# A hybrid attention trunk on one core: PSUM banks, squares, splits and token loads between the first feed-forward and the second attention

## The chip, the cores and the metric

The kernel runs on one core of a Trainium2 chip. The time is the device time of one execution in microseconds (us); lower is better. The core's engines work in parallel, each on its own list of instructions, strictly in the order in which they were issued: PE (matrix products, writes to the eight banks of PSUM), DVE, ACT and POOL (elementwise work), and SP, which only issues transfers (DMA). An instruction that depends on another engine waits at the head of its engine's list, and everything behind it waits too.

## The reference, cut to what matters

Two layers, each an attention and a gated feed-forward with a convolution, on 1024 latent tokens and 256 context tokens of width 1024. Only the passage from the end of layer 0 to the attention of layer 1 matters here:

```python
x = x + gt2 * conv_ffn(h, ...)                     # end of layer 0
h  = modulate(rmsnorm(x, g_attn[i]), sh1, sc1)     # layer 1: norm over 1024 features, scale and shift
hc = modulate(rmsnorm(ctx, g_attn[i]), sh1c, sc1c)
q, k, v    = attn_inputs(h, w_in, gq, gk, n_kv)             # products with the QKV weights, norm of q and k
_, k_c, v_c = attn_inputs(hc, w_in, gq, gk, n_kv, with_q=False)
o = sliding_window_attention(apply_rope(q), apply_rope(k), v, k_c, v_c, sink)
```

All of it is float32. The kernel keeps that accuracy by splitting every factor into a high part (rounded to the multiplier's format) and a low part (the difference), and by adding three products: high by high, high by low, low by high. So each operand costs a copy to the high part, mostly on ACT (`hi`), and a subtraction for the low part, on DVE or POOL (`lo`).

## The kernel before, in words

**Who sets the order.** Each phase is planned as a list of operations by the class `Sched`: an operation names its engine, a guessed duration, what it reads and writes, a `key` (the lower goes first among those that are ready) and the buffers that it takes and releases (`acq`, `rel`). `run()` plays this through with guessed durations and latencies and then issues all instructions in the order found; `InOrder` ties each engine to it. An operation with `port=True` on DVE is not planned to overlap one on POOL. Nothing is decided on the chip: a bad guess shows as a wait. The first feed-forward (`ffn(0, ...)`, whose last part is planned in `plan_next`) and the second attention are planned separately, one after the other. The second begins its plan at time 0 with what the first left; `NREADY` is the guess of when the sums of squares of the second token half are there.

**Tiling.** Features lie on the 128 partitions in eight tiles `k`, tokens along the free axis in two halves of 512 (halves 0 and 1) and the 256 context tokens. The second half is finished last.

**End of the feed-forward.** The last products of the down-projection accumulate in four PSUM banks (`dn`), finished one after another by the last 24 matmuls. DVE adds each bank, scaled, into two tiles of the residual (`xn<-dn`, eight instructions of 128x512, `plan_ev`); each result is written to memory (`x_dram<-xn`, `plan_xd`) and squared on ACT (`sq`), and DVE adds the eight squares into `sums`. Meanwhile four pieces of the context's key and value weights arrive (`ckv`, 512 KB each, into the ring `raw` of three buffers) and are split (`whi` on ACT, `wlo` on DVE).

**Start of the second attention.** A new set of PSUM tiles is laid over the same eight banks (`s` three, `pt` two, `mm` two, `pv` one), in the order in which they are first asked for. PE first computes the context's keys and values (`plan_ctx_kv`: 48 matmuls `mm<-whi,h1chi` of 128x512), then the mean square of the second half (`mp`, `pt<-invd,sums`), then the QKV products of four 128-token blocks of the first half (96 matmuls of 128x384, `mm<-whi,h1hi`, `plan_sw_qkv`), whose weights come in four pieces `slab` (384 KB, also in the ring `raw`, split like the others), then those of four blocks of the second half. For the second half `plan_norm` computes the factor 1/sqrt of the mean square (`n1v` DVE, `n1y` POOL, Newton steps on DVE), spreads it over a diagonal tile (`S<-idr,n1y`), has PE broadcast it (`bc`, `pt<-S,ones`), copies it out of PSUM (ACT), multiplies the tokens by it (`t<-x,modc,S`, eight on DVE), adds the shift and rounds (`h1hi<-t`, ACT), and takes the low part (`n1lo`, eight on DVE). The tokens of that half come back from memory (`x<-x_dram`, four transfers of 512 KB).

Each block's product is copied from its bank by ACT into one of two buffers `qraw`; q and k are normed from it (`qsq` ACT, `qv` DVE, `qy` POOL, `qt`, `qy`, `qn` DVE), which frees the buffer. The `mm` banks are two, so the product of block n+2 waits for the copy of block n. Score products (`s`), softmax and the products with V (`pv`) of one head group then run between the QKV products of the next.

Of the kernel before, what the change touches and what calls it, by code (L numbers as in the profile page):

```python
# [11 lines left out]
F32 = mybir.dt.float32  # L12
# [5 lines left out]
P = 128  # L18
D = 1024
KT = 8  # L20
# [206 lines left out]
def trunk_kernel(ctx, tc, xperm, xseq, cc, wmod, bmod, gnorm, na_wqkv, na_gq, na_gk, na_bias, na_wo,  # L227
# [87 lines left out]
    def lo_part(nm, dt=F32R):  # L315
        return hpool.tile([P, 2, 512], dt, tag="hlo", name=nm, bufs=8)
# [319 lines left out]
    def plan_norm(sc, l, psa, wk, sums, x, hl, key):  # L636
# [5 lines left out]
        if l == 0:  # L642
            for k in range(KT):
                def sq(e, k=k):
                    if k:
                        B["sq"] = wk.tile([P, 512], F32, tag="ptlo", name="sq", bufs=PTB)
                    act.activation(B["sq"] if k else sums[:, :n], x[:, k, :], AF.Square)

                def add(e, k=k, B2=B):
                    ENG[e].tensor_tensor(out=sums[:, :n], in0=sums[:, :n], in1=B2["sqs", k], op=ALU.add)  # L650

                def sq2(e, k=k, f=sq):
                    f(e)
                    B["sqs", k] = B.get("sq")
                sc.op("act", t_act(n), sq2, reads=[("x1", k)], writes=[K("sq", k)] if k else [K("sums")], key=key,
                      acq=[("ptlo", K("sq", k), 1)] if k else ())
                if k:
                    sc.op(("pool", "dve"), (t_pool(n), t_dve(n)), add, reads=[K("sq", k), K("sums")], writes=[K("sums")],
                          key=key, rel=[K("sq", k)])
        else:  # L660
            sc.op("x", NREADY, lambda e: None, writes=[K("sums")], key=key - 1)

        def mp(e):
            B["mp"] = psa("pt", F32)
            for i in range(nt):
                pe.matmul(B["mp"][:, i:i + 1], sums[:, i * P:(i + 1) * P], invd, start=True, stop=True)
        sc.op("pe", 0.4, mp, reads=[K("sums")], writes=[K("mp")], key=key, acq=[("pt", K("mp"), 1)], rel=["sums1"])

# [25 lines left out]
        sc.op("pe", 0.86, bc, reads=[K("dg")], writes=[K("bcp")], key=key, acq=[("pt", K("bcp"), 1)], rel=[K("dg")])  # L694
# [4 lines left out]
        sc.op("act", t_actp(n), bs, reads=[K("bcp")], writes=[K("bc")], key=key, acq=[("S", K("bc"), KT)], rel=[K("bcp")])  # L699
        los = []  # L700
        for k in range(KT):
            hi = hl[0][:, k, :]

            def mul(e, k=k):
                B["t", k] = wk.tile([P, 512], F32, tag=("pthi", "ptlo")[k % 2], name="t", bufs=PTB)
                dve.scalar_tensor_tensor(out=B["t", k][:, :n], in0=x[:, k, :], scalar=modc[:, l, 0, 1, k:k + 1], in1=B["bc"][:, :n],
                                         op0=ALU.mult, op1=ALU.mult)
            sc.op("dve", t_dve(n), mul, reads=[K("bc"), ("x1", k)], writes=[K("t", k)], key=key, rel=[K("bc")],
                  acq=[(("pthi", "ptlo")[k % 2], K("t", k), 1)])

            def hif(e, k=k, hi=hi):
                act.activation(hi, B["t", k][:, :n], AF.Identity, bias=modc[:, l, 0, 0, k:k + 1])
            sc.op("act", t_act(n), hif, reads=[K("t", k)], writes=[K("hi", k)], key=key)

            def lof(e, k=k, hi=hi):
                if k % 2 == 0:
                    hl[1].tiles[k // 2] = lo_part("n1lo")
                dve.scalar_tensor_tensor(out=hl[1][:, k, :], in0=B["t", k][:, :n], scalar=modc[:, l, 0, 0, k:k + 1],
                                         in1=hi.bitcast(F32), op0=ALU.add, op1=ALU.subtract)
            los.append((k, lof))  # L720
            if k % 2 == 0:
                continue
            for k, lof in los[-2:]:
                sc.op("dve", t_dve(n), lof, reads=[K("hi", k), K("t", k // 2 * 2 + 1)], writes=[(f"h{l}", 1, k)], key=key, rel=[K("t", k)])

# [245 lines left out]
    NWAIT = (2, 3, 4)  # L971
    NREADY = 7.0
    NPRE = 3
# [276 lines left out]
    def ffn(l, opj, xt1, todo):  # L1250
# [756 lines left out]
        if not last:  # L2007
            plan_next(sc, KS, xn, bank, x_tile, plan_sums, plan_bc, plan_t, plan_hilo, u_done)
        sc.run()
# [13 lines left out]

    def plan_next(sc, KS, xn, bank, x_tile, plan_sums, plan_bc, plan_t, plan_hilo, u_done):

# [65 lines left out]
        plan_sums("n1", 512, lambda k: xn(1, k), lambda k: ("xn", 1, k), lambda k: KS[5],  # L2091
                  lambda k: [("xnt", 1, k // 2)], sums, "sq")
        for i in range(4):
# [10 lines left out]
            def lo(e, i=i):  # L2104
                dve.tensor_tensor(out=CW[i][1], in0=CW[i, "r"], in1=CW[i][0].bitcast(F32), op=ALU.subtract)
            sc.op("dma", 1.8, load, reads=[("dw", 4, FT // 2 - 4, "r")], writes=[("slr", i)], key=KS[5] - 4,
                  acq=[("raw", ("slr", i), 2)])
            sc.op("act", t_act(1024), hi, reads=[("slr", i), ("dw", 4, FT // 2 - 1, "wl", 0)],
                  writes=[("slh", i)], key=key, acq=[("w", ("slw", i), 1)], rel=[("slr", i)])
            sc.op("dve", t_dve(1024) + 0.03, lo, reads=[("slr", i), ("slh", i)], writes=[("sll", i)], key=key, rel=[("slr", i)])  # L2110

# [22 lines left out]
    def plan_ctx_kv():  # L2134
# [3 lines left out]
        for i in range(4):  # L2138
            def mm(e, i=i):
                for tt in range(2):  # L2140
                    if i == 0:
                        acc[tt] = psa("mm", F32)
                    sl = slice(tt * P, tt * P + P)
                    for k in (2 * i, 2 * i + 1):
                        wh, wl = [a[:, k % 2 * 512:k % 2 * 512 + 512] for a in CW[i]]
                        for m, (a, w) in enumerate(((hh, wh), (hl, wh), (hh, wl))):
                            pe.matmul(acc[tt], a[:, k, sl], w, start=(k == 0 and m == 0), stop=(k == KT - 1 and m == 2))
            sc.op("pe", 12 * t_pe(512), mm, writes=[("ckv", "acc")], key=-300,
                  acq=[("mm", ("ckv", "acc", tt), 1) for tt in range(2)] if i == 0 else (), rel=[("cw", i)])
        for tt in range(2):  # L2150
            def cp(e, tt=tt):
                R[tt] = wk.tile([P, 672], F32, tag="S", name="S", bufs=SBUFS)
                act.activation(R[tt][:, :512], acc[tt], AF.Copy)
            r = ("ckv", "raw", tt)
            sc.op("act", t_actp(512), cp, reads=[("ckv", "acc")], writes=[r], key=-250, acq=[("S", ("ckv", "S", tt), 4)],
                  rel=[("ckv", "acc", tt)])
# [88 lines left out]
    def plan_sw_qkv(n):  # L2245
# [14 lines left out]
        plan_rstd(sc, key, J, c0, nh, wk, 320)  # L2260
        vk, qk = ("v", g, tt), ("q", g, tt)
# [17 lines left out]
        sc.op("dve", t_dve(nh * DH), qn, reads=[K("raw"), K("y")], writes=[K("qn")], key=key,  # L2279
              acq=[("qn", K("qn"), 2)], rel=[K("raw")])  # L2280
# [179 lines left out]

    for j in range(0, KT, 2):
        dma.dma_start(xs[1].tiles[j // 2], x_dram[:, (KT + j) * 512:(KT + j + 2) * 512].rearrange("p (k t) -> p k t", k=2))
    h[1] = [hpool.tile([P, KT, 512], F32R, tag="hhi", name="h1hi", bufs=2), Parts([None] * 4, 2)]
    sc.hold("raw", "sums1", 1)
    for i in range(4):
        sc.hold("w", ("cw", i), 1)
    plan_ctx_kv()
    plan_norm(sc, 1, psa, wk, sums1, xs[1], h[1], -100)
    for g in range(NKV):
# [167 lines left out]
```

## Time and profile before

| | |
|---|---|
| three executions | 2819.53, 2819.89, 2821.8 us; median 2819.89 |
| profiled execution | 2819.35 us, of which the traced span is 2817.6 us |
| granted clock of PE over the span | 0.995 of full speed |
| DVE, ACT, POOL busy | 2288.3 (81%), 1687.3 (60%), 394.4 us (14%) |

The passage lies between 1655 and 1720 us of the span. In the timeline a row gives the start, the length, the engine, the operation as out<-in with its tile names, the shape, the number of instructions merged into the row, and in brackets how long the engine sat idle before it and what ended that. "SPq" is the issuing of a transfer. A wait is put down to one releaser, the one that came last by the profile. In the table of windows each row is a stretch of time with each engine's busy time, PE's granted clock, the share of time that the DMA engines were busy, and GB/s.

### The profile page before, as it was taken

What the parts mean: (1) busy time and instruction counts of PE and PEld (TensorE: products, weight loads), DVE (VectorE), ACT (ScalarE), POOL (GpSimd) and SP (SyncE); (2) the same over time, 40 slices, a digit from 0 to 9 for tenths busy, and PEclk for the clock granted to TensorE, in tenths of its full rate; (3) what the DMA queues carried; (4) which work ended last, traced back from release to release, by engine and by line L of the source; (5) the groups of instructions that cost most, each with busy time, mean ns of one, the idle gap of its engine ahead of it and who ended that gap; (6) DMA issues with size and microseconds to landing.
All of it is one profiled execution on the core that took longest, in us unless ns stands there. A gap on an engine that the chain in (4) does not pass through costs nothing. (4 is left out here: it accounts for less than half of the span.)

```text
span 2817.6 us, 45649 instructions
## 1 busy us (share of the span) xinstructions
PE 2758.1 (98%) x16205; PEld 2427.5 (86%) x16205; DVE 2288.3 (81%) x5013; ACT 1687.3 (60%) x3312; POOL 394.4 (14%) x652
## 2 busy tenths in 40 slices
PE   6999999999999999999999999999999999999999
PEld 5999999999889987777788878999987788888887
DVE  7888878889688687778797788888988888888757
ACT  5877777778456554444454457888864555455443
POOL 1222212223000000000010006455420000000000
PEclk9999999999999999999999999999999999999999
DMA  6232222224645544444376561010263322334745
GB/s 250 64 97 81 72 70 82 89 77 145 238 146 187 185 162 139 153 144 161 135 257 199 172 213 33 13 37 19 81 203 128 124 104 99 113 108 145 252 150 180
DMA packets 144295, 373.54 MB, mean 133 GB/s; under 512 B 22081, under 2 KB 35009, under 8 KB 142657
## 3 DMA queue, kind: packets, MB, share of 16 engines
q1 hardware_dynamic: 144064, 370.60, 39.5%
q8 instruction: 128, 2.10, 0.3%
q14 instruction: 103, 0.84, 0.1%
HBM read 303.50 MB, written 67.04 MB: 132 GB/s over the span
## 5 line engine op out<-in xcount | busy, mean ns | idle before, releaser
L51 ACT ACTIVATE whi<-wraw 128x512 fp32r<-128x512 f32 (+1 forms) x264 | 212.3, 805 | 202.8 <-PE uc L51 62.3
L51 DVE TENSOR_TENSOR wlo<-wraw,whi 128x512 fp32r<-128x512 f32 (+1 forms) x264 | 239.5, 909 | 45.0 <-ACT whi L51 44.5
L51 DVE TENSOR_TENSOR ptlo<-pt,pthi 128x512 fp32r<-128x512 f32 (+2 forms) x384 | 223.4, 596 | 56.3 <-ACT pthi L51 52.4
L51 PE MATMUL dn<-ghi,whi 128*128 128x512 f32 x616 | 243.8, 396 | 0.0
L51 PE MATMUL dn<-ghi,wlo 128*128 128x512 f32 x616 | 242.8, 394 | 0.0
L51 PE MATMUL dn<-glo,whi 128*128 128x512 f32 x616 | 242.0, 393 | 0.0
L51 ACT ACTIVATE S<-S,m 128x640 f32<-128x640 f32 (+3 forms) x288 | 220.6, 767 | 23.1 <-DVE m L51 17.7
L51 ACT ACTIVATE pthi<-pt 128x512 fp32r<-128x512 f32 (+2 forms) x384 | 194.3, 523 | 66.6 <-PE pt L51 58.2
L51 DVE SCALAR_TENSOR_TENSOR u<-c,cv,u 128x1023 f32<-128x1023 f32 x176 | 223.2, 1280 | 6.9 <-ACT u L51 5.8
L51 ACT ACTIVATE whi<-s 128x1024 fp32r<-128x1024 f32 (+1 forms) x120 | 113.2, 943 | 191.3 <-PE uc L51 133.9
L51 ACT ACTIVATE ghi<-graw 128x512 fp32r<-128x512 f32 x154 | 96.5, 631 | 192.5 <-PE dn L51 108.3
L51 PE MATMUL pt<-idr,S 128*128 128x128 f32 x1280 | 193.8, 273 | 3.2 <-DVE ptlo L51 2.0
L51 PE MATMUL mm<-whi,h0hi 128*128 128x384 f32 x512 | 181.6, 355 | 0.4 <-ACT qraw L51 0.4
L51 DVE TENSOR_TENSOR glo<-graw,ghi 128x512 fp32r<-128x512 f32 x154 | 105.6, 689 | 83.8 <-ACT ghi L51 76.1
L51 PE MATMUL mm<-wlo,h0hi 128*128 128x384 f32 x512 | 172.3, 337 | 0.0
L51 DVE TENSOR_TENSOR wlo<-s,whi 128x1024 fp32r<-128x1024 f32 (+1 forms) x120 | 129.7, 1081 | 40.8 <-ACT whi L51 40.7
L51 PEld LDWEIGHTS pt<-idr,S 128*128 128x128 f32 x1280 | 151.0, 140 | 12.1 <-DVE ptlo L51 2.9
L51 POOL TENSOR_TENSOR n1y<-n1v,mhalf 128x4 f32<-128x4 f32 (+1 forms) x9 | 9.2, 1023 | 993.1 <-DVE n1v L51 993.1
L51 PE MATMUL ua<-t12hi,whi 128*128 128x512 f32 x352 | 138.7, 394 | 5.5 <-ACT t12hi L51 4.0
L51 POOL TENSOR_TENSOR qy<-qv,mhalf 128x4 f32<-128x4 f32 (+1 forms) x112 | 119.6, 1068 | 155.6 <-DVE qv L51 136.6
L51 PEld LDWEIGHTS dn<-ghi,wlo 128*128 128x128 f32 x616 | 115.5, 187 | 28.4
L51 PEld LDWEIGHTS dn<-glo,whi 128*128 128x128 f32 x616 | 115.5, 188 | 27.5
(347 smaller groups left out, 8759.3 us busy)
## 6 DMA issues: line engine op xcount, KB each, us to landing
wraw<-in_w_up_dram SPq DMA_DIRECT2D x132, 512.0 KB, 3.5
wm<-in_wmod_dram SPq DMA_DIRECT2D x80, 512.0 KB, 4.2
wraw<-in_w_down_dram SPq DMA_DIRECT2D x44, 512.0 KB, 3.6
graw<-g_dram SPq DMA_DIRECT2D x44, 512.0 KB, 4.4
wraw<-in_w_down_dram SPq DMA_DIRECT2D x88, 256.0 KB, 3.2
graw<-g_dram SPq DMA_DIRECT2D x66, 256.0 KB, 2.8
slab<-in_na_wqkv_dram SPq DMA_DIRECT2D x32, 384.0 KB, 3.8
woraw<-in_na_wo_dram SPq DMA_DIRECT2D x24, 512.0 KB, 4.1
```

Source lines behind the costliest of these rows:

```text
L51: r = f(*a, **k)
```

## The change

Cut to its core:

```diff
 plan_norm, second half (l == 1)
-            sc.op("x", NREADY, lambda e: None, writes=[K("sums")], key=key - 1)
+            sc.op("late", NREADY, lambda e: None, writes=[K("sums")], key=key - 1)
...
-        sc.op("pe", 0.4, mp, ..., key=key, ...)
+        sc.op("pe", 0.4, mp, ..., key=key - 300 * l, ...)
...
+        tag = ("pt", "s")[l]
-            B["bcp"] = psa("pt", F32)
+            B["bcp"] = psa(tag, F32)
...
-        sc.op("act", t_actp(n), bs, ...)
+        if l == 0:
+            sc.op("act", t_actp(n), bs, ...)
+        f = K(("bc", "bcp")[l])
...
+            off = l == 1 and k % 2 == 1
...
+                act.activation(t if off else hi, t, AF.Identity, bias=modc[:, l, 0, 0, k:k + 1])
+                if off:
+                    act.activation(hi, t, AF.Copy)
...
+                if off:
+                    pool.tensor_tensor(out=hl[1][:, k, :], in0=B["t", k][:, :n], in1=hi.bitcast(F32), op=ALU.subtract)
+                    return
...
-    NREADY = 7.0
+    NREADY = 8.0
 ffn, plan_ev (evictions of dn)
-                reads=[("dn", d, m)], writes=[("xn", c, k)], key=key, rel=[("d" + d, m)])
+                reads=[("dn", d, m)], writes=[("xn", c, k)], key=key, rel=[("d" + d, m)], port=False)
 plan_next
+        for n, k in enumerate(k + 4 * i for k in range(4) for i in range(2)):
+            ring = ("raw", "sq", "g")[(n % 2 + 1) * (n > 0)]
...
-                dve.tensor_tensor(out=CW[i][1], in0=CW[i, "r"], in1=CW[i][0].bitcast(F32), op=ALU.subtract)
-            sc.op("dma", 1.8, load, ..., key=KS[5] - 4, ...)
+                ENG[e].tensor_tensor(out=CW[i][1], in0=CW[i, "r"], in1=CW[i][0].bitcast(F32), op=ALU.subtract)
+            sc.op("dma", 1.8, load, ..., key=KS[5] - (24 if i == 3 else 4), ...)
...
-            sc.op("dve", t_dve(1024) + 0.03, lo, ..., key=key, ...)
+            sc.op(*(("pool", 2.28) if i < 2 else ("dve", t_dve(1024) + 0.03)), lo, ..., key=key + 30 * (i == 3), ...)
 second attention
-    sc = Sched(CAPS)
+    sc = Sched(dict(CAPS, qraw=3))
...
-            J["raw"] = wk.tile([P, 384], F32, tag="qraw", name="qraw", bufs=2)
+            J["raw"] = wk.tile([P, 384], F32, tag="qraw", name="qraw", bufs=3)
...
-    for j in range(0, KT, 2):
-        dma.dma_start(xs[1].tiles[j // 2], x_dram[...]...)
...
+    for tag in ("s", "pt"):
+        psa(tag, F32)
     plan_ctx_kv()
-    plan_norm(sc, 1, psa, wk, sums1, xs[1], h[1], -100)
+    for j in range(0, KT, 2):
+        sc.op("dma", 1.2, lambda e, j=j: dma.dma_start(xs[1].tiles[j // 2], ...), writes=[("x1", j), ("x1", j + 1)], key=-206)
+    plan_norm(sc, 1, psa, wk, sums1, xs[1], h[1], -260)
```

In words: the tiles `s` and `pt` are asked for first, so `mm` gets other banks. The eight squares go to two rings of buffers (`sq` and the `ghi` ring) in the order in which the banks finish, instead of one ring. Two of the four `ckv` low parts go to POOL, and so does one `slab`'s; the fourth `ckv` load moves up. The four token loads become planned operations behind the first two slabs. The mean-square product `mp` moves ahead on PE, the broadcast `bc` stays in a bank of the ring `s`, and the multiplication reads it there, without ACT's copy. For the odd tiles ACT writes the shifted token back and then rounds it (two instructions), and POOL takes the low part. `qraw` has three buffers. The context's products are planned per 128-token block.

On PE, at the first matmuls of the second attention, the last rows of the down-projection are followed by the context's products:

```order
 L51 MATMUL dn<-ghi,wlo 128x512
-L51 MATMUL mm<-whi,h1chi 128x512 [waits DVE_49,Activation_49]
+L51 MATMUL mm<-whi,h1chi 128x512 [waits Activation_49]
 L51 MATMUL mm<-whi,h1clo 128x512
-L51 MATMUL mm<-wlo,h1chi 128x512
+L51 MATMUL mm<-wlo,h1chi 128x512 [waits Pool_49]
```

The first of them no longer waits for DVE; the third now waits for POOL's low part.

On DVE, from the last evictions of the down-projection (`xn<-dn`) to the sums of squares:

```order
+L51 SCALAR_TENSOR_TENSOR xn<-dn,modc,xn 128x512 x7
+L51 TENSOR_TENSOR wlo<-ckv,whi 128x1024
 L51 SCALAR_TENSOR_TENSOR xn<-dn,modc,xn 128x512
-L51 TENSOR_TENSOR wlo<-ckv,whi 128x1024 x2
-L51 SCALAR_TENSOR_TENSOR xn<-dn,modc,xn 128x512 x3
+L51 TENSOR_TENSOR sums_19594<-sums_19594,sq 128x512 x2
 L51 TENSOR_TENSOR wlo<-ckv,whi 128x1024
-L51 SCALAR_TENSOR_TENSOR xn<-dn,modc,xn 128x512 x2
-L51 TENSOR_TENSOR wlo<-ckv,whi 128x1024
-L51 SCALAR_TENSOR_TENSOR xn<-dn,modc,xn 128x512 x2
-L51 TENSOR_TENSOR sums_19575<-sums_19575,sq 128x512 x7
+L51 TENSOR_TENSOR sums_19594<-sums_19594,sq 128x512 x5
```

Two splits have left DVE, the evictions stand together, and one split has moved between the sums; two splits of slabs and then `n1v` follow in both programs.

On PE, at the QKV products of the first block with the first slab (`h1lo_19176` is the low part of the tokens for slab 0, `h1lo_19177` for slab 1):

```order
 L51 MATMUL mm<-whi,h1lo_19176 128x384
 L51 MATMUL mm<-wlo,h1hi_19175 128x384
+L51 MATMUL s<-S,ones 128x128 [waits DVE_49] x4
 L51 MATMUL mm<-whi,h1hi_19175 128x384
 L51 MATMUL mm<-whi,h1lo_19177 128x384
```

The broadcast now stands behind 6 of the 128x384 matmuls; before, it stood behind 24. The mean-square product `mp`, before behind all 48 context matmuls, now stands behind 36 of them. On SP the eight writes `x_dram` come first, then two slabs, then the four token loads, then the other slabs; before, the first slab stood behind four of the writes, a token load between the last writes, the second slab behind them, and three token loads ahead of the third slab. The order of the feed-forward of layer 1 is unchanged on all engines.

More of the change, by code (lines that the diff above doesn't have):

```diff
@@ L723, in plan_norm @@
             for k, lof in los[-2:]:
-                sc.op("dve", t_dve(n), lof, reads=[K("hi", k), K("t", k // 2 * 2 + 1)], writes=[(f"h{l}", 1, k)], key=key, rel=[K("t", k)])
+                sc.op(*(("pool", t_pool(n)) if l == 1 and k % 2 else ("dve", t_dve(n))), lof, reads=[K("hi", k), K("t", k // 2 * 2 + 1)], writes=[(f"h{l}", 1, k)], key=key, rel=[K("t", k)])
     class Oproj:
@@ L2104, in lo @@
             def lo(e, i=i):
-                dve.tensor_tensor(out=CW[i][1], in0=CW[i, "r"], in1=CW[i][0].bitcast(F32), op=ALU.subtract)
-            sc.op("dma", 1.8, load, reads=[("dw", 4, FT // 2 - 4, "r")], writes=[("slr", i)], key=KS[5] - 4,
+                ENG[e].tensor_tensor(out=CW[i][1], in0=CW[i, "r"], in1=CW[i][0].bitcast(F32), op=ALU.subtract)
+            sc.op("dma", 1.8, load, reads=[("dw", 4, FT // 2 - 4, "r")], writes=[("slr", i)], key=KS[5] - (24 if i == 3 else 4),
                   acq=[("raw", ("slr", i), 2)])
@@ L2138, in plan_ctx_kv, with mm @@
         for i in range(4):
[L2139 to L2149, printed above, removed]
+            def mm(e, tt, i=i):
+                if i == 0:
+                    acc[tt] = psa("mm", F32)
+                sl = slice(tt * P, tt * P + P)
+                for k in (2 * i, 2 * i + 1):
+                    wh, wl = [a[:, k % 2 * 512:k % 2 * 512 + 512] for a in CW[i]]
+                    for m, (a, w) in enumerate(((hh, wh), (hl, wh), (hh, wl))):
+                        pe.matmul(acc[tt], a[:, k, sl], w, start=(k == 0 and m == 0), stop=(k == KT - 1 and m == 2))
+            for tt in range(2):
+                sc.op("pe", 6 * t_pe(512), lambda e, tt=tt, f=mm: f(e, tt), writes=[("ckv", "acc", tt)], key=-300,
+                      acq=[("mm", ("ckv", "acc", tt), 1)] if i == 0 else (), rel=[("cw", i)])
         for tt in range(2):
@@ L2154, in plan_ctx_kv @@
             r = ("ckv", "raw", tt)
-            sc.op("act", t_actp(512), cp, reads=[("ckv", "acc")], writes=[r], key=-250, acq=[("S", ("ckv", "S", tt), 4)],
+            sc.op("act", t_actp(512), cp, reads=[("ckv", "acc", tt)], writes=[r], key=-250, acq=[("S", ("ckv", "S", tt), 4)],
                   rel=[("ckv", "acc", tt)])
```

55 lines of the change are left out of this document (36 added, 19 removed).

## The prediction

> **What bounds the kernel now.** I read the page first, for the busiest engine, then the list of PE's waits.
>
> ```profile
> PE 2758.1 (98%) x16205; PEld 2427.5 (86%) x16205; DVE 2288.3 (81%) x5013; ACT 1687.3 (60%) x3312; POOL 394.4 (14%) x652
> ```
>
> ```profile
> PE mm L51 <- ACT qraw L51: 5.3, 2, 4.9
> PE mm L51 <- ACT sq L51: 3.5, 1, 3.5
> ```
>
> PE has work nearly always, so a change on another engine pays only by a wait of PE that it removes. The change touches the passage that holds these two, the longest of the middle of the kernel: one of 3.5 us, one of 4.9. The windows around them show a second cost beside each.
>
> ```profile
> 1670.00:1680.00 10.00, 10.00 (x39) 8.07 (x38) 8.40 (x12) 4.74 (x7) 0.00 (x0) 0.83 0.86 289
> 1700.00:1710.00 10.00, 5.07 (x23) 4.75 (x22) 7.99 (x23) 3.23 (x9) 5.42 (x9) 0.75 0.01 2
> ```
>
> The granted clock, the third number from the end, falls to 0.83 and 0.75. PE's timeline gives both waits, the slow stretches and the costs of the work between:
>
> ```profile
> 1665.80 0.39 PE L51 MATMUL dn<-ghi,wlo 128*128 128x512 f32 x1
> 1669.64 0.47 PE L51 MATMUL mm<-whi,h1chi 128*128 128x512 f32 x1 [3.45 <-ACT sq L51]
> ...
> 1671.20 0.63 PE L51 MATMUL mm<-whi,h1chi 128*128 128x512 f32 x1
> ...
> 1674.51 0.40 PE L51 MATMUL mm<-wlo,h1chi 128*128 128x512 f32 x1
> ...
> 1682.23 0.95 PE L51 MATMUL pt<-invd,sums 128*128 128x1 f32 x8
> 1683.04 0.42 PE L51 MATMUL mm<-whi,h1hi 128*128 128x384 f32 x1
> ...
> 1687.30 1.05 PE L51 MATMUL pt<-S,ones 128*128 128x128 f32 x8
> ...
> 1702.20 0.34 PE L51 MATMUL mm<-wlo,h1hi 128*128 128x384 f32 x1
> 1707.47 0.69 PE L51 MATMUL mm<-whi,h1hi 128*128 128x384 f32 x1 [4.93 <-ACT qraw L51]
> ...
> 1712.03 0.34 PE L51 MATMUL mm<-wlo,h1hi 128*128 128x384 f32 x1
> ```
>
> From 1674.51 to 1682.23 lie 34 context matmuls: 0.23 us each. From 1671.20 to 1674.51 lie 8: 0.41 each. From 1683.04 to 1687.30 lie 24 QKV matmuls: 0.1775 each. From 1707.47 to 1712.03 lie 14: 0.326 each. So the slow clock cost 8 x 0.18 = 1.5 us after the first wait and 14 x 0.148 = 2.1 after the second. What each waited for:
>
> ```profile
> 1668.08 1.41 DVE L51 SCALAR_TENSOR_TENSOR xn<-dn,modc,xn 128x512 f32<-128x512 f32 x2
> ...
> 1702.14 1.40 DVE L51 SCALAR_TENSOR_TENSOR n1lo<-t,modc,h1hi 128x512 fp32r<-128x512 f32 x2
> ...
> 1706.32 0.49 DVE L51 TENSOR_TENSOR qn<-qraw,qy 128x320 f32<-128x320 f32 x1
> ```
>
> ```profile
> 1706.92 0.49 ACT L51 ACTIVATE qraw<-mm 128x384 f32<-128x384 f32 x1 [4.73 <-DVE qy L51]
> ```
>
> The first ends when DVE's eviction at 1668.08 to 1669.49 is over: the first `mm` bank is one of the four `dn` banks, and DVE put three splits between the evictions. The profile names ACT, but the program's first matmul waits for DVE too, and the bank can only come from there. The second ends when the third QKV product can be copied out of its bank. ACT has no free `qraw` until DVE's `qn`, which stands behind the eight low parts `n1lo`, the last at 1702.14.
>
> **The change part by part.** *Banks.* The first matmul of the new program does not wait for DVE. It needs the first split:
>
> ```profile
> 1659.71 1.06 ACT L51 ACTIVATE whi<-ckv 128x1024 fp32r<-128x1024 f32 x1 [0.68 <-DMA ckv<-in_sw_ckv_dram]
> 1662.26 1.06 ACT L51 ACTIVATE whi<-ckv 128x1024 fp32r<-128x1024 f32 x1 [1.49 <-DMA ckv<-in_sw_ckv_dram]
> ```
>
> ```profile
> L51 POOL TENSOR_TENSOR wlo<-woraw,whi x3: 2407/2410/3914, 669.6 to 703.7; 128x1024 fp32r<-128x1024 f32 x3
> ```
>
> POOL has not split a `ckv`; the same shape took it 2.41 to 3.91 us. The two low parts are ready by 1663.2 and 1665.7, at worst 1664.7 and 1668.6. PE needs them at 1666.7 and 1669.4, so this is hidden either way. The whole 3.45 goes, and with it the 1.5 of slow clock.
>
> *Squares and mean.* PE reaches `mp` at 1666.19 + 36 x 0.23 = 1674.5. DVE's durations, by groups over 1660 to 1720:
>
> ```profile
> L51 DVE SCALAR_TENSOR_TENSOR n1lo<-t,modc,h1hi 128x512 fp32r<-128x512 f32 x8 | 5.8, 760 | 0.0
> L51 DVE SCALAR_TENSOR_TENSOR t<-x,modc,S 128x512 f32<-128x512 f32 x8 | 5.8, 744 | 0.0
> L51 DVE SCALAR_TENSOR_TENSOR xn<-dn,modc,xn 128x512 f32<-128x512 f32 x8 | 5.6, 748 | 2.2 <-PE dn L51 2.2
> L51 DVE TENSOR_TENSOR sums<-sums,sq 128x512 f32<-128x512 f32 x7 | 4.8, 691 | 0.6
> L51 DVE TENSOR_TENSOR wlo<-ckv,whi 128x1024 fp32r<-128x1024 f32 x4 | 4.8, 1220 | 0.0
> ```
>
> The seventh eviction starts when PE finishes the last bank, at 1666.2. Behind it stand a split, an eviction, two sums, a split and five sums: 0.75 + 1.22 + 0.75 + 1.38 + 1.22 + 3.46 = 8.8, so the sums are there at 1675.0. PE waits 0.5; 0 if the rows overlap a little, 0.8 with POOL at its slowest, since ACT's first square waits for POOL's second split.
>
> *Broadcast.* `bc` is now early on PE, and DVE's part of it stands behind the splits of slabs 0 and 1. Slab 1's load takes the buffer that the last `ckv` split frees, at 1671.6 by the sum above. What a slab costs:
>
> ```profile
> L51 ACT ACTIVATE whi<-slab x48: 829/845/872, 34.0 to 1934.8; 128x768 fp32r<-128x768 f32 x48
> L51 DVE TENSOR_TENSOR wlo<-slab,whi x36: 939/952/972, 34.9 to 1688.5; 128x768 fp32r<-128x768 f32 x36
> ...
> L51 POOL TENSOR_TENSOR wlo<-slab,whi x12: 1837/1849/1929, 1730.8 to 1936.5; 128x768 fp32r<-128x768 f32 x12
> ...
> DMA to landing us min/median/max: 2.8/3.6/18.9
> ```
>
> The four slabs of this passage, each asked for by itself, landed in 3.5 to 6.1 us (the first and the third):
>
> ```profile
> DMA to landing us min/median/max: 3.5/3.5/3.5
> ...
> DMA to landing us min/median/max: 6.1/6.1/6.1
> ```
>
> ```profile
> 1683.22 0.16 DVE L51 TENSOR_SCALAR n1v<-pt 128x4 f32<-128x4 f32 x1 [3.10 <-PE pt L51]
> ...
> 1686.37 0.87 DVE L51 TENSOR_SCALAR S<-idr,n1y 128x128 f32<-128x128 f32 x4
> ```
>
> ```profile
> 1683.46 1.01 POOL L51 TENSOR_TENSOR n1y<-n1v,mhalf 128x4 f32<-128x4 f32 x1 [69.32 <-DVE n1v L51]
> ```
>
> Slab 1 lands at 1675.1 to 1677.7 and is split 1.8 later. From `n1v` to the end of the diagonal I take 2.6 to 3.1 us: 1.25 to the end of `n1y`, three small steps as long as `n1v` (0.5, or 1.0 with the waits between them), 0.87. So `bc` can go at 1679.5 to 1682.6. PE arrives at 1675.0 + 0.81 (`mp`, 1682.23 to 1683.04) + 12 x 0.23 + 6 x 0.1775 = 1679.6. The wait is 0 to 3.0; I take 1.2, a landing of 4.5, as fewer bytes are queued ahead of this load than of the 6.1.
>
> *Third and fourth slab.* They wait for the buffers of slabs 0 and 1 and stand behind the token loads. The fourth starts at 1677.9, lands in 3.5 to 6.1, and needs 0.85 and POOL's 1.85: 1684.1 to 1686.7. PE needs it at 1679.6 + 1.2 + 0.8 + 23 x 0.1775 = 1685.7. The wait is 0 to 1.0, or 2.5 if slab 1 was late as well; I take 0.3.
>
> *Second half.* PE comes to it at 1681.6 + 90 x 0.1775 + 0.3 = 1697.9. DVE now has eight products, four low parts and a split behind `bc`: 6.0 + 3.0 + 1.0 and under 1 us of small work, done by 1692.5. POOL's four low parts I price by two bounds, twice a DVE one (1.5) and half of its 128x1024 split at its slowest (2.0); they end by 1695, and PE needs the last at 1701. This is hidden, with 6 us of cover; without it the wait of 4.93 would stay in part. The third `qraw` lets the third copy go without `qn`. The fourth needs `qn` of the first block, which came 3.3 after the end of the last low part (1703.54 to 1706.81). With 1.7 of context work ahead it comes near 1700, and PE needs that bank at 1697.9 + 4.3 = 1702.2. So 4.93 and 2.1 go too.
>
> *Attention.* Its order is planned anew. PE's waits there, 1718 to 2110, make 5.2 us in eight rows, of which the first and the last are:
>
> ```profile
> PE pv L51 <- DVE osb L51: 2.4, 3, 1.1
> ...
> PE pt L51 <- DVE qv L51: 0.2, 1, 0.2
> ```
>
> At most 5 are to be had, and as much again may be lost; I take 0.4 lost.
>
> *Sum.* 3.45 + 1.5 + 4.93 + 2.1 = 12.0 removed, 0.5 + 1.2 + 0.3 + 0.4 = 2.4 added: 9.6 gained. The profiled execution took 2819.35, so 2809.8; the median of the runs is 0.5 above it, so 2810.3.
>
> [...]
>
> **The rivals.** *Half of it (0.17).* `bc` waits its 3.0 and the fourth slab 0.6 and the clock falls once: 0.5 + 3.0 + 0.6 + 1.5 + 0.4 = 6.0 added, 6.0 gained, 2813.9. For it: 6.1 us landings in this very passage, and 0.86 DMA share. Against: before `bc`, only 0.39 + 0.39 MB follow the writes.
>
> *Given back (0.08).* PE is early at the scores, but DVE is not, and PE waits there for what it gained at the second wait: 9.6 - 7.0 = 2.6 gained, 2817.3. Speaking for it, POOL takes over some 12 us (two splits of 2.4, one of 1.85, four of 1.5), and if they hold DVE up, DVE comes later. Against it, over the whole attention DVE has slack:
>
> ```profile
> 1718.70:2000.00 281.30, 279.57 (x2068) 274.37 (x2068) 245.25 (x820) 238.15 (x604) 151.80 (x318) 1.00 0.10 26
> ```
>
> DVE is busy 245 of 281 us, PE 280: DVE can follow a PE that is 10 us earlier.
>
> *Better (0.08).* The new order also loses some 3 us of the attention's 5.2: 2807.3.
>
> *Slower (0.05).* PE, DVE and the slabs form one chain at `bc`: a late slab 1 stops DVE, DVE stops PE, and nothing else may pass. At the longest landing of a slab, 18.9 us, `bc` goes at 1671.6 + 18.9 + 1.8 + 2.9 = 1695.2. PE then stands 15.6, and the clock costs 2.1 more: 17.7 + 0.5 + 0.4 added against 12.0, 2826.5. It decides from a landing near 12 us. Against: this passage's slabs took half of that.
>
> That the first matmul still waits is excluded, since POOL's slowest split is 2.0 us early.
>
> **How the numbers follow.** The forecast has 0.62, with a range of its own of 2807 to 2814. About 0.2% (5.6 us: below 2814.2 or above 2825.5) is what a measurement here can tell. Faster: 0.61 of the forecast, 0.12 of half of it, 0.08 and 0.01 of given back, 0.82. Slower by that much: only the last, and a worse attention, 0.06. Between: 0.12. The range, 2806.5 to 2815.5, leaves out the slower case, most of given back and the tails.
>
> **What would show it.** In the new profile: no wait of PE at the first context matmul and granted clock 1.00 from 1660 to 1680 (banks); waits below 1 us at `mp` and near 1.2 at the broadcast (chain), named for DVE; the first second-half matmul near 1698 with no wait for `qraw`; the first scores some 10 us earlier than before and still so at the end of the attention. I am wrong if PE stands over 3 us at the broadcast, if a slow stretch remains, or if the lead of 10 us at the scores is smaller at 2000.

## The result, and the profile after

| | before | after |
|---|---|---|
| median of six executions each, on one chip | 2820.22 us | 2809.43 us (2809.0 to 2809.64) |
| ratio | | 0.9962, 95% interval 0.9952 to 0.9972 |
| profiled execution, traced span | 2819.35, 2817.6 us | 2809.03, 2807.3 us |

The change gains 10.8 us in the medians and 10.3 in the profiled executions; the forecast was 2810.3. First the busy engines on the page, and the windows of the two stretches that the prediction opened with:

```profile
PE 2755.6 (98%) x16205; PEld 2426.1 (86%) x16205; DVE 2281.2 (81%) x4990; ACT 1689.7 (60%) x3315; POOL 413.6 (15%) x675
```

```profile
1700.00:1710.00 10.00, 10.00 (x67) 9.86 (x67) 7.76 (x24) 6.29 (x16) 6.87 (x15) 1.00 0.01 2
1670.00:1680.00 10.00, 9.50 (x49) 7.91 (x48) 8.43 (x19) 4.69 (x9) 1.01 (x1) 1.00 0.99 353
```

In the stretch from 1700 PE is busy for 10.00 of 10 us where it was 5.07, and the granted clock (third number from the end) is 1.00 in both stretches, where it was 0.83 from 1670 and 0.75 from 1700. What PE still waits for between 1655 and 1705, and the places in its timeline:

```profile
PE mm L51 <- ACT whi L51: 0.7, 1, 0.7
PE pt L51 <- DVE sums L51: 0.5, 1, 0.5
PE mm L51 <- DVE wlo L51: 0.4, 1, 0.4
```

```profile
1665.88 0.40 PE L51 MATMUL dn<-ghi,wlo 128*128 128x512 f32 x1
1666.11 0.39 PE L51 MATMUL mm<-whi,h1chi 128*128 128x512 f32 x1
...
1674.95 1.05 PE L51 MATMUL pt<-invd,sums 128*128 128x1 f32 x8 [0.50 <-DVE sums L51]
...
1679.78 1.05 PE L51 MATMUL s<-S,ones 128*128 128x128 f32 x8
...
1683.12 0.44 PE L51 MATMUL mm<-whi,h1hi 128*128 128x384 f32 x1 [0.73 <-ACT whi L51]
...
1684.12 0.44 PE L51 MATMUL mm<-wlo,h1hi 128*128 128x384 f32 x1 [0.38 <-DVE wlo L51]
...
1698.27 0.33 PE L51 MATMUL mm<-whi,h1hi 128*128 128x384 f32 x1
1698.44 0.33 PE L51 MATMUL mm<-whi,n1lo 128*128 128x384 f32 x1
```

The context's products follow the down-projection without a gap, `mp` waits 0.5, the broadcast not at all, the third slab costs 0.73 + 0.38, and the second half begins at 1698.27 with no wait for `qraw`.

For what follows I measure one stretch: from the start of the last matmul of the down-projection to the start of the last `oacc<-o1hi` matmul of the second attention. The second row below is the kernel before, the first the changed one; the last number ahead of the semicolon is the end of the stretch.

```profile
L51 PE MATMUL oacc<-o1hi,whi x128: 389/389/478, 763.5 to 2147.0; 128*128 128x512 f32 x128
```

```profile
L51 PE MATMUL oacc<-o1hi,whi x128: 389/389/478, 763.4 to 2157.0; 128*128 128x512 f32 x128
```

2157.0 - 1665.80 = 491.2 before, 2147.0 - 1665.88 = 481.1 after: 10.1 of the 10.3 us lie in this stretch. It is a better measure of a single profile than the span, since the program's start varies: the first `uc` matmul of the first feed-forward came between 808.2 and 812.2 in the fourteen profiles, while from there to the start of the last down-projection matmul all took 856.99 to 857.03.

### The profile page after: what moved, and what is told of

The parts are those of the page before. It is cut to its first block, busy times and chain, and to the rows that moved or that the text cites. A ratio compares the mean times of both kernels' runs of the same rounds, so it can differ in the third digit from the quotient of the medians.

```text
span 2807.3 us, 45623 instructions
## 1 busy us (share of the span) xinstructions
PE 2755.6 (98%) x16205; PEld 2426.1 (86%) x16205; DVE 2281.2 (81%) x4990; ACT 1689.7 (60%) x3315; POOL 413.6 (15%) x675
## 4 chain that ended last, share of the span: by engine, by line
PE 70%; DVE 3%; ACT 1%; DMA 1%; issue 1%; POOL 0%; DVEq 0%; SPq 0%; ACTq 0%
PE ua L51 17%; PE dn L51 15%; PE uc L51 13%; PE mm L51 6%; PE ud L51 4%; PE oacc L51 4%; PE pt L51 3%; PE pv L51 3%; PE s L51 2%; PE dnc L51 2%; PE mod L51 1%; DVE S L51 1%; DVE x L51 0%; DVE wlo L51 0%; DVE ptlo L51 0%
```

## The experiments

All start from the changed kernel, except banks alone, which starts from the kernel before. The number behind a name is that of the experiment. The ratio is to the kernel before on the same chip; the stretch is that of the one profiled execution.

| run | median us | ratio, 95% interval | stretch us |
|---|---|---|---|
| changed again (5) | 2810.05 | 0.9964, 0.9950 to 0.9977 | 480.9 |
| banks undone (1) | 2811.06 | 0.9965, 0.9953 to 0.9978 | 483.3 |
| banks alone, from before (2) | 2820.03 | 0.9999, 0.9990 to 1.0007 | 492.1 |
| POOL undone (6) | 2813.46 | 0.9975, 0.9965 to 0.9984 | 484.7 |
| banks and POOL undone (10) | 2812.67 | 0.9975, 0.9966 to 0.9985 | 487.9 |
| `qraw` two (7) | 2812.77 | 0.9973, 0.9963 to 0.9984 | 487.2 |
| norm late (8) | 2810.16 | 0.9964, 0.9951 to 0.9976 | 483.2 |
| `qraw` two and norm late (9) | 2816.96 | 0.9991, 0.9982 to 0.9999 | 487.9 |
| tokens first (3) | 2816.01 | 0.9985, 0.9976 to 0.9993 | 486.4 |
| last token behind third slab (4) | 2810.72 | 0.9965, 0.9952 to 0.9979 | 482.5 |
| `mp` later (11) | 2820.60 | 1.0005, 0.9996 to 1.0014 | 493.1 |
| passage clean (12) | 2820.46 | 1.0003, 0.9994 to 1.0012 | 492.5 |

The profiled execution is not always a typical one: that of changed again is the fastest of its five, those of `qraw` two and of banks and POOL undone are the slowest of their seven and ten. Some parts of the change were not undone by themselves, among them the two rings for the squares and the broadcast that is read in PSUM without ACT's copy; what they are worth is not shown.

### The measure

> The changed kernel itself, run beside the next three on one chip, as their measure. In its first profile the stretch from the last matmul of the down-projection to the last matmul oacc<-o1hi of the second attention took 481.1 us (491.2 in the kernel before). If the waits of the attention behind the first scores are a property of the kernel, it takes 480.8 to 481.5 again; if they vary from execution to execution, as 483.4 with the banks undone suggests (1.7 of it waits for pthi that no other run had), it may lie 1 to 2 us off.

The stretch took 480.9 (2146.6 against 1665.73), 0.2 less than the first time. That it repeats so closely is in part luck, since a wait inside did not: the 1.1 us at the third slab was 0.2 this time, so the rest of the stretch took 0.7 more. The list of waits between 1655 and 1705:

```profile
PE pt L51 <- DVE sums L51: 0.5, 1, 0.5
PE mm L51 <- DVE wlo L51: 0.2, 1, 0.2
```

So a difference of about one microsecond between two single profiles says nothing by itself; where it is the slab or the attention, the named wait and the median decide.

### The first stall: bank or order of DVE's work?

```diff
-    for tag in ("s", "pt"):
-        psa(tag, F32)
```

> The changed kernel without its first request for tiles of s and pt, so that mm lies again over banks that DVE has to empty; every engine's order is the same otherwise. Theory A (the bank was the whole cause of the first stall): the wait of 3.5 us is back at the first context matmul, and the slow clock behind it, 1.5: 4 to 5 us slower than the changed kernel. Theory B (the bank and DVE's splits between the evictions made it together): the evictions now stand in one row, the sixth ends near 1666.1 and the eighth at 1668.85, so PE waits 0 to 0.4 at the first matmul and at most 1.5 at the seventh, and no slow stretch follows: 0.2 to 2 us slower.

PE's only new wait in the passage is this:

```profile
1666.74 0.47 PE L51 MATMUL mm<-whi,h1chi 128*128 128x512 f32 x1 [0.21 <-DVE xn L51]
```

Theory B holds in the passage: 0.2 us and no slow clock (the context matmuls behind it follow each other by 0.23 us). The other 2 us of this profile's stretch are attention: 1.7 of it stood on `pthi` in two waits. The ratio, 0.9965, lies within the intervals of the changed kernel. So the bank order, in the changed kernel, is worth next to nothing.

The same two lines added to the kernel before:

> The kernel before with the first request for tiles of s and pt, and nothing else. Theory A (each stall is worth its own 5.0 and 7.0 us): 5 us faster than before, 2815. Theory B (what PE gains at the first stall it gives back further on, because the third slab and DVE's second-half work are no earlier): the first wait is gone, a wait of 2 to 4 us stands at the third slab's low part (in the kernel before it is ready at 1688.1, and PE would now need it near 1682.2), the wait for qraw stays, and the gain is 0 to 2.5 us.

Its three longest waits between 1666 and 1712:

```profile
PE mm L51 <- ACT qraw L51: 4.9, 1, 4.9
PE mm L51 <- ACT S L51: 1.6, 1, 1.6
PE mm L51 <- DVE wlo L51: 0.4, 1, 0.4
```

The wait of 3.45 is gone, and the gain is nil (ratio 0.9999). PE comes to the QKV products earlier, stands 1.6 where ACT cannot empty a `mm` bank because it stands itself for the load of slab 1 (1.47), runs 3.4 us at half clock after that (0.50 from 1683.16 to 1686.57), and then stands its 4.9 for `qraw` as before. Theory B, with the new wait at another spot than I had said. Removed alone, this stall only moved PE up to the next things that were not earlier.

Undoing POOL's parts brings DVE's splits back between the evictions, and the low parts of the odd tiles back to DVE:

```diff
-            off = l == 1 and k % 2 == 1
+            off = False
...
-            sc.op(*(("pool", 2.28) if i < 2 else ("dve", t_dve(1024) + 0.03)), lo, ...)
+            sc.op("dve", t_dve(1024) + 0.03, lo, ...)
```

> The changed kernel with POOL's parts given back: the two ckv low parts and the four odd token low parts on DVE, and ACT again with one instruction per odd tile. Theory A (POOL's help is what lets DVE keep up): the sums are ready 2.4 us later (two times 1.22), PE stands 2.9 at the mean square instead of 0.5, the clock falls for a window (1.5), and the fourth copy into qraw comes up to 3 later: 2.4 to 7 us slower than the changed kernel. Theory B (DVE gets slower while POOL works, so POOL's help is given back): less than 1 us slower.

```profile
1676.79 1.25 PE L51 MATMUL pt<-invd,sums 128*128 128x1 f32 x8 [2.65 <-DVE sums L51]
```

The wait at the mean square is 2.65 instead of 0.50 (2.9 expected), and one slow stretch of 3.4 us follows (clock 0.50 from 1677.51 to 1680.92). In the medians it is 3.4 us slower than changed again, though the intervals of the two ratios overlap. Theory A, at its lower end: the fourth `qraw` copy did not come late. With banks and POOL undone together:

> The changed kernel with the bank order and POOL's parts undone at once, so that DVE's splits stand between the evictions again and mm lies over banks that DVE has to empty. With POOL undone alone PE stood 2.7 at the mean square, with the banks undone alone 0.2 at the context. Theory A (the two waits stand one behind the other on one chain, DVE's work up to the sums, and do not add): the first wait is 3 to 3.5, the one at the mean square goes to 0 to 0.3, and the stretch is 485 to 486.5 (484.7 with POOL undone alone). Theory B (they add): the first wait of 3.5 comes on top of the 2.7, 488 to 490.

```profile
1669.98 0.77 PE L51 MATMUL mm<-whi,h1chi 128*128 128x512 f32 x1 [3.44 <-DVE xn L51]
```

The first stall is back at its old size, and the mean square behind it waits for nothing: 3.44 and 0 here, 0 and 2.65 before. The ratios of the two kernels agree, 0.9975. The two waits are the same delay of DVE, taken early or late, as theory A has it. The stretch that I had given with theory A, 485 to 486.5, was too short: it took 487.9, near the 488 of theory B. The clock was at half for 6.83 us, from 1669.10 to 1675.93, instead of 3.41, and this execution, the slowest of its ten, stood 4.6 us for `pthi` in the attention. So it is the two waits and the medians that speak for A, and not the stretch.

So the first stall has two cures, the bank order or a DVE list with fewer splits between the evictions, and only the second also makes the sums earlier, which is where the gain at this place comes from.

### The second stall: which of its three cures?

```diff
-    sc = Sched(dict(CAPS, qraw=3))
+    sc = Sched(CAPS)
...
-            J["raw"] = wk.tile([P, 384], F32, tag="qraw", name="qraw", bufs=3)
+            J["raw"] = wk.tile([P, 384], F32, tag="qraw", name="qraw", bufs=2)
```

> The changed kernel with two buffers of qraw instead of three. Theory A (the third buffer is needed, as the prediction has it): the third copy waits for the first block's qn, about 1700.6, so the first block of the second half, which needs that bank near 1698, stands 2 to 3.5, perhaps with a slow stretch of 1.5: 2 to 5 us slower than the changed kernel. Theory B (the plan draws qn and other PE work forward, and the early second half alone removes the stall): within 1 us.

No wait for `qraw` stands in its passage; the plan put three groups of transposes ahead of the second half instead, with one wait of 0.9. It is 2.7 us slower in the medians, with overlapping intervals. Its profile shows 2.9 at the third slab, with a slow stretch behind it (0.50 from 1686.78 to 1690.19), and 3.3 for `osb` in the attention (1.1 in the changed kernel). The slab's wait cannot be put down to the edit: the slab landed late behind the same orders (last section). So theory A's mechanism, a wait for `qraw`, is refuted; that the second buffer costs more than the 1 us of theory B is not shown.

```diff
-    plan_norm(sc, 1, psa, wk, sums1, xs[1], h[1], -260)
+    plan_norm(sc, 1, psa, wk, sums1, xs[1], h[1], -100)
...
-        sc.op("pe", 0.4, mp, ..., key=key - 300 * l, ...)
+        sc.op("pe", 0.4, mp, ..., key=key, ...)
```

> The changed kernel with mean square and broadcast back at their old places on PE (behind 48 context matmuls and 24 of the QKV matmuls, instead of 36 and 6). Theory A (the early norm removes the second stall): the broadcast comes 4.7 us later, the last low part near 1698, the fourth copy into qraw waits for qn until 1704.9, and PE stands 2 to 3 there, less the 0.5 that it no longer waits at the mean square: 1.5 to 4 us slower. Theory B (three buffers of qraw and POOL's low parts are enough without it): within 0.7 us of the changed kernel, or faster by the 0.5.

```profile
PE mm L51 <- ACT qraw L51: 1.5, 2, 1.2
PE mm L51 <- DVE wlo L51: 0.4, 1, 0.4
```

1.5 us of the wait for `qraw` return, 0.5 at the mean square and 0.7 at the slab go, no slow clock (most 128x384 matmuls behind both waits took 0.33 to 0.35 us), and the median is that of changed again: theory B. The stretch of this one profile is 2.3 us longer, most of it in the attention, whose order is planned anew. Both undone:

> The changed kernel with two of its parts undone at once: two buffers of qraw, and mean square and broadcast at their old places. Each alone left no wait of 4.9 at the second half (none for qraw with two buffers, 1.2 with the late norm). Theory A (each of the parts is enough by itself, so only together are they missed): the third copy waits for the first block's qn, near 1704.5, PE stands 4 to 6 before the second half, the clock falls for one or two windows (1.5 to 2.1), and the stretch from the last down-projection matmul to the last oacc matmul takes 486.5 to 489 (481.0 in the changed kernel, 491.2 before). Theory B (POOL's low parts alone keep DVE early enough): a wait below 2, no slow stretch, 482 to 484.

```profile
1703.86 0.69 PE L51 MATMUL mm<-whi,h1hi 128*128 128x384 f32 x1 [3.96 <-ACT qraw L51]
```

Now the second stall is back, 3.96 of its 4.93, with a slow stretch behind it (the 128x384 matmuls took 0.52 us up to the one at 1706.26, 0.34 from 1706.83 on), and the ratio is 0.9991 instead of 0.9964. Theory A. The third buffer and the early norm replace each other; POOL's part alone does not do it.

### The order of the loads

```diff
+    for j in range(0, KT, 2):
+        dma.dma_start(xs[1].tiles[j // 2], x_dram[...]...)
     h[1] = ...
...
-    for j in range(0, KT, 2):
-        sc.op("dma", 1.2, lambda e, j=j: dma.dma_start(xs[1].tiles[j // 2], ...), ..., key=-206)
```

> The changed kernel with its four token loads issued ahead of the first slab instead of behind the second; all other engines keep their order. Theory A (the queue matters): the loads wait on SP for the writes of the same tokens, slab 0 is issued near 1673.6 instead of 1669.3 and lands behind 2 MB, near 1678; DVE comes to the broadcast's diagonal 3 to 5 us later, and PE stands 3 to 5 us at the first slab and at the broadcast together: 3 to 6.5 us slower than the changed kernel, with a slow stretch at the upper end. Theory B (DMA is full from 1665 to 1680 in either order, and PE's context matmuls cover it): less than 1 us slower.

Its waits between 1668 and 1720:

```profile
PE mm L51 <- ACT S L51: 3.0, 1, 3.0
PE pt L51 <- DVE sums L51: 0.5, 1, 0.5
PE s L51 <- DVE S L51: 0.3, 1, 0.3
```

```profile
1682.78 1.82 ACT L51 ACTIVATE whi<-slab 128x768 fp32r<-128x768 f32 x2 [8.55 <-DMA slab<-in_sw_wqkv_dram]
```

ACT stood 8.55 us for the first slab, and PE 3.0 behind it for the copy that empties its bank; the clock was at 0.50 from 1684.14 to 1687.55 and the 128x384 matmuls took at least 0.52 us up to the one at 1690.58, 0.33 from 1691.12 on. That is 5.3 us of the stretch, and a ratio of 0.9985, outside the interval of the changed kernel: theory A. Of the parts undone singly this one has the highest ratio, though its interval overlaps those of POOL undone and `qraw` two.

The other way, the last of the four token loads behind the third slab:

> The changed kernel with the last of the four token loads issued behind the third slab instead of ahead of it; nothing else moves on any engine. Theory A (the 1.1 us that PE stands at the third slab come from the 2 MB of tokens ahead of it in the queues): the slab lands 1.0 to 1.4 us earlier, PE's two waits of 0.73 and 0.38 go, 0.6 to 1.1 us faster than the changed kernel. Theory B (the landing is set by when the buffer falls free, 1675.8): within 0.3 us. Theory C (the last tokens then come too late for DVE, or the fourth slab's low part on POOL becomes the next wait): 0.3 to 1.5 us slower or no gain.

The third and fourth slab's first splits, in the changed kernel and in this one (its clock runs 0.57 us later, by the last down-projection matmul at 1666.45):

```profile
1682.23 0.84 ACT L51 ACTIVATE whi<-slab 128x768 fp32r<-128x768 f32 x1 [2.71 <-DMA slab<-in_sw_wqkv_dram]
...
1683.59 0.83 ACT L51 ACTIVATE whi<-slab 128x768 fp32r<-128x768 f32 x1
```

```profile
1682.08 0.85 ACT L51 ACTIVATE whi<-slab 128x768 fp32r<-128x768 f32 x1 [2.04 <-DMA slab<-in_sw_wqkv_dram]
...
1684.42 0.85 ACT L51 ACTIVATE whi<-slab 128x768 fp32r<-128x768 f32 x1 [0.88 <-DMA slab<-in_sw_wqkv_dram]
```

```profile
1687.22 0.44 PE L51 MATMUL mm<-wlo,h1hi 128*128 128x384 f32 x1 [0.90 <-POOL wlo L51]
```

The third slab was split 0.7 us earlier than in the changed kernel's first profile, and PE's 0.73 there is gone. But in its second profile, with no edit, that split came earlier still (15.13 us after the last down-projection matmul, against 15.63 here and 16.35 in the first), so this gain can be chance. What neither of those two profiles has is the wait for the fourth slab: it came 0.3 later than in the first, and PE stood 0.90 for its low part on POOL. That fits theory C, that what one slab gains the next pays with the DMA engines busy (0.99 of 1670 to 1680 in the changed kernel), but one profile does not show it; the ratio, 0.9965, shows no gain.

### Two attempts at a better kernel

```diff
-    NREADY = 8.0
+    NREADY = 8.6
```

> The changed kernel with a later guess for the sums (8.6 instead of 8.0), which puts the mean square behind 42 of the context matmuls instead of 36 and the broadcast behind 15 of the QKV matmuls instead of 6; the attention's order is planned anew behind it. If the wait of 0.5 at the mean square, the same in all runs of that order, comes from the place alone, it goes and nothing takes its place up to the second half: 0.3 to 0.7 us of the passage. What the new order of the attention does I cannot tell from these runs: 1 to 2 us either way, so the whole may be 1.5 faster or as much slower than the changed kernel.

The wait at the mean square went, as expected. But:

```profile
1697.11 0.75 PE L51 MATMUL pt<-idr,st 128*128 128x128 f32 x4 [14.00 <-ACT st L51]
```

What ended this wait was ACT's `st`, rounded from the context's normed keys `S` that DVE had just made:

```profile
1694.92 1.48 DVE L51 TENSOR_TENSOR S<-S,gqk 128x256 f32<-128x256 f32 x1
...
1696.43 0.63 ACT L51 ACTIVATE st<-S 128x512 fp32r<-128x512 f32 x1 [2.03 <-DVE S L51]
```

PE's list here has the transposes of `st` ahead of the third slab's matmuls, and both are late for one reason, DVE's list. In the changed kernel the third slab's low part stands ahead of the first product `t`; here it stands behind the whole norm, as `S` does, and ends 0.5 us after `st`:

```profile
1683.10 0.96 DVE L51 TENSOR_TENSOR wlo<-slab,whi 128x768 fp32r<-128x768 f32 x1 [2.91 <-ACT whi L51]
1683.98 2.72 DVE L51 SCALAR_TENSOR_TENSOR t<-x,modc,s 128x512 f32<-128x512 f32 x4
```

```profile
1681.56 2.72 DVE L51 SCALAR_TENSOR_TENSOR t<-x,modc,s 128x512 f32<-128x512 f32 x4 [1.51 <-PE s L51]
...
1696.65 0.94 DVE L51 TENSOR_TENSOR wlo<-slab,whi 128x768 fp32r<-128x768 f32 x1
```

The norm's operations have the key -260 and the slabs' splits -202, and of those that may start the lower goes first. In the changed kernel's plan the split may start just ahead of the first `t`, and goes. With the guess 0.6 us later POOL has an instruction of the context's norm (`ckvy`) in the plan at that moment, which the split may not overlap (`port`) and the products may; they go first, and eight products and four low parts keep DVE from then on. That is read from the planner's rules and the two lists. A lower key for the splits might be the cure; it was not tried, and it would have to bring PE's matmuls of the third slab ahead of the transposes as well. ACT had rounded the slab by 1682.6, so the 14 us are the plan's alone. The clock fell as well, to 0.50 for 13.65 us, from 1688.14 to 1701.79.

> The later mean square of the run before, the last token load behind the third slab, and the fourth slab's low part on DVE instead of POOL. If the waits left in the passage (0.5 at the mean square, 0.2 to 1.1 at the third slab, 0.9 at the fourth when the third came early) are each where the runs put them, none is left above 0.4, the passage is 1 to 1.5 us shorter than in the changed kernel, and the stretch from the last down-projection matmul to the last oacc matmul takes 479.3 to 480.2, with 1 to 2 either way for the attention's new order. If DVE cannot carry the extra 0.95 us, the wait moves to the first low parts of the second half.

```profile
1693.57 0.69 PE L51 MATMUL mm<-wlo,h1hi 128*128 128x384 f32 x1 [10.69 <-DVE wlo L51]
```

It is the same split behind the same norm, and here PE stands for the split itself, 10.7 us. That hides what the other two edits do. Both lost all that the change had gained.

## Why the prediction was right, point by point

*Sum.* 12.0 removed and 2.4 added were forecast, 9.6 gained. The 12.0 went entirely: neither wait nor slow stretch is left in the passage (granted clock 1.00 from 1655 to 1720). Added were 0.5 + 0.73 + 0.38 = 1.6 there, which leaves 10.4; the stretch gained 10.1, so the attention gave back 0.3. In the second execution the passage added 0.7 and the attention gave back 0.9, so 1.9 and 1.6 were added in all where 2.4 was forecast, but not in the same places. Undoing the cures of a stall together gave back 3 us for the first (ratio 0.9975, experiment 10) and 7.6 for the second (0.9991, experiment 9), where 5.0 and 7.0 were forecast.

*First stall.* Right in size, wrong in credit. "The first matmul of the new program does not wait for DVE" is true, but with the banks undone it waited 0.2. The step that failed is the equation of the 3.45 with the bank order: DVE's shorter list before the sums is what carries the gain, the bank order alone gains nothing.

*Mean square.* Arrival at 1674.5 and sums at 1675.0 were forecast, a wait of 0.5; PE started it at 1674.95 after 0.50.

*Broadcast.* PE's arrival was forecast for 1679.6 and was 1679.78. The term of 1.2 was mis-sized: it was 0. The second slab was split by ACT from 1675.02, where I had its landing at 1676.1 (it took 3.6 us from its issue, where I had taken 4.5), and the diagonal was ready at 1679.53:

```profile
1678.65 0.88 DVE L51 TENSOR_SCALAR S<-idr,n1y 128x128 f32<-128x128 f32 x4
```

*Third and fourth slab.* The heading named both, the working priced only the fourth, at 0.3. The wait was at the third, 1.1 in one execution and 0.2 in another. The miss at the broadcast and the one here offset each other: 1.5 forecast for slabs and broadcast, 1.1 measured.

*Second half.* Forecast 1697.9, measured 1698.27, with no wait. POOL's last low part ended at 1696.45 instead of 1695, still ahead of the second half. The text let the early norm and the third `qraw` buffer each carry a part of the 4.93; with the early norm alone no wait for `qraw` was left (experiment 7), with the third buffer alone 1.5 (experiment 8). POOL's low parts, without which the prediction had a part of the 4.93 stay, were not needed for it: with them on DVE (experiment 6) PE does not wait for `qraw` in the passage either.

*Attention.* 0.4 lost was forecast; 0.3 came in one execution and 0.9 in the other, so the size is in part luck. One landmark failed: the first scores came 3.75 us earlier (1714.95 for 1718.70), not 10. The new plan puts 225 matmuls of context and QKV ahead of them instead of 192, and 33 of 0.1775 are 5.9 us. The lead was there, the landmark had moved. At the end of the attention it is 10.0.

*Rivals.* "Half of it" and "given back" did not come. "Slower" did not come either, but chains of its kind (DVE late, PE behind it, nothing passes) came in three experiments. In experiment 3 the first slab landed late, DVE stood 5.45 for its split and PE 3.3 in two waits. In experiments 11 and 12 it was no landing but the plan: PE stood 14.0 for `st` and 10.7 for the third slab's low part, where the rival had 15.6 at the broadcast. One number in the plan, moved by 0.6 us, was enough for that.

## What to carry to other kernels

Before crediting a gain to one edit, undo it alone, and undo it together with its neighbours: a stall can have two cures, and two stalls can be one delay. Count a removed wait only up to the next resource that is not earlier. In a planned order, look for an instruction on the critical chain whose place hangs on a guess or a key, since a shift of 0.6 us in a guess moved one by 13 us here.

## What the runs showed of the hardware

*When the clock falls.* Slow stretches lasted 3.41 us (1670.97 to 1674.38), 6.83 (1705.10 to 1711.92) and 10.24 (2176.14 to 2186.38) in the kernel before and 13.65 in experiment 11: one, two, three and four times 3.413. Rows of 3.41 us, counted from the start of a slow stretch, with PE's busy time (the second number of time) and the granted clock: three of the kernel before, two of the banks alone, two of the tokens first.

```profile
1664.14:1667.55 3.41, 2.05 (x9) 1.31 (x7) 3.41 (x5) 2.19 (x4) 0.00 (x0) 1.00 0.77 258
1667.55:1670.97 3.42, 1.33 (x6) 1.15 (x7) 3.42 (x5) 1.59 (x2) 0.00 (x0) 1.00 0.86 260
1670.97:1674.38 3.41, 3.41 (x10) 2.63 (x9) 3.10 (x6) 1.48 (x3) 0.00 (x0) 0.50 0.99 328
```

```profile
1679.75:1683.16 3.41, 1.85 (x13) 1.77 (x13) 1.67 (x4) 2.77 (x7) 0.79 (x1) 1.00 0.92 310
1683.16:1686.57 3.41, 3.41 (x13) 3.41 (x12) 2.62 (x10) 0.26 (x1) 2.39 (x3) 0.50 1.02 408
```

```profile
1680.73:1684.14 3.41, 1.41 (x7) 0.83 (x5) 0.49 (x1) 1.23 (x2) 0.00 (x0) 1.00 0.82 326
1684.14:1687.55 3.41, 2.29 (x6) 1.78 (x6) 2.17 (x7) 3.38 (x8) 1.01 (x1) 0.50 0.54 157
```

After a row with 2.05 us of work the clock stayed at 1.00; after 1.85 (which counts eight matmuls of one column as work), 1.41 and 1.33 the next row ran at 0.50. So here it fell after a row that was busy for 54%, and stayed after one of 60%. The sum of busy time does not decide alone: in experiment 11 the clock stayed after a row with 1.80 us of work (1681.31 to 1684.73), less than the 1.85. Behind the single waits of 1.56 (banks alone) and 2.65 (POOL undone) stood a slow stretch of 3.41, behind the 1.2 of the late norm none; in the kernel before, such a stretch cost 1.5 (eight matmuls at 0.41 instead of 0.23). There PE had been at work for 1.33 us when the slow stretch began (second row).

*DVE beside POOL.* In experiment 11 the low part `n1lo`, 0.75 us by itself (at 1691.58), took 1.78 while POOL split a slab, and it ended 0.54 after POOL's instruction:

```profile
1684.48 1.78 DVE L51 SCALAR_TENSOR_TENSOR n1lo<-t,modc,h1hi 128x512 fp32r<-128x512 f32 x1 [0.20 <-ACT h1hi L51]
```

```profile
1683.91 1.81 POOL L51 TENSOR_TENSOR wlo<-slab,whi 128x768 fp32r<-128x768 f32 x1 [2.15 <-ACT whi L51]
```

In the changed kernel four products `t`, which read one operand from PSUM, took 2.72 (0.68 each, the row at 1683.98 above), as in experiment 11 with POOL at rest for most of them (the row at 1681.56), while POOL worked on the same kind of split:

```profile
1684.62 1.85 POOL L51 TENSOR_TENSOR wlo<-slab,whi 128x768 fp32r<-128x768 f32 x1
```

So POOL's low part was not free for DVE here: 1.78 instead of 0.75 for the one `n1lo` beside it.

*Landings.* With the same orders on all engines up to there, the third slab landed 6.4, 5.2 and 8.6 us after its issue, and its split began 16.35, 15.13 and 18.54 us after the last down-projection matmul (changed kernel, again, two `qraw`). So a wait behind this transfer, with the DMA engines busy 0.99 of 1670 to 1680 in the changed kernel, is here a range of 3 us and not a number.
